# Up projection of a hybrid decoder layer: the low halo moves into the high row, and twelve matmuls of 258 columns become eight of 260 and four of 256

## The chip, the core and the metric

The kernel runs on one core of one Trainium2 chip. The metric is the device time of one execution in microseconds, as the median of several runs: 1258.69 us here (three runs, 1258.04 to 1259.17). Profiles are taken by the hardware profiler in an execution of their own.

## What is computed

One decoder layer for 1024 tokens and 16 meta tokens of width 1024, in float32. Ahead of the change stand the input projection, a convolution branch, windowed attention, their merge and a layer norm that gives `h`. The change lies in the feed-forward part:

```python
D_FF, FFN_TAPS = 2816, 3
up = causal_dwconv(h @ ffn_w_up, ffn_dw, ffn_dw_b)      # (T, 2 * D_FF), 3 taps along the tokens
u, g = jnp.split(up, 2, axis=-1)
f = (jax.nn.gelu(g, approximate=False) * u) @ ffn_w_down
return layer_norm(DEEPNORM_ALPHA * h + f, ln2_g, ln2_b)
```

The convolution is causal with 3 taps: an output at token t needs the projection at t, t - 1 and t - 2. A block of tokens therefore carries two extra columns in front, the halo.

## The kernel before

**Arithmetic.** Every float32 operand x is split into a high part, `hi = round(x)` to TensorE's reduced float32 format, and a low part, `lo = x - hi`. A product of two operands is three matmuls: high weight times high activation, high weight times low activation, low weight times high activation (`ah, hi`; `ah, lo`; `al, hi`). The weight is the stationary operand (128 x 128), the activation the moving one (128 channels x columns of tokens); the sum over channels is collected in PSUM.

**Up projection (the loop from L1550 on).** For each of 22 chunks `c` of 128 up channels and the 128 gate channels beside them, a 2 x 2 block product is made with seven block products instead of eight, the way Strassen and Winograd have it. The blocks of the weights are gate and up channels by the two halves of the 1024 contraction channels; the blocks of the activations are those halves by the two halves of the tokens. The seven moving operands (`B11, B21, BT2, BT4, BT1, BT3, B22`, sums and differences of the activation's blocks) are formed and split once and stay in SBUF; the seven weight operands are formed and split anew for every chunk, a few products ahead (`w_ahead(9)`, `wsplit` L1393 and L1394, sums in `up_weights` L1411).

A half of the tokens is 514 columns wide (`HW`): 2 of halo and 512. It is cut into two column groups, `SUB = [(0, 258), (258, 514)]`: group 0 has the halo and 256 tokens, group 1 has 256 tokens. Each of the seven products (`prod`, matmuls at L1572) goes over group 0 and then group 1: for each of four contraction chunks `k` the three terms `j`, so 12 matmuls of 258 columns and then 12 of 256. The four PSUM tiles `V4, X, Z, Y` (named pw, px, pz, py in the profile) have 1024 columns, two banks of 512 each; group 0 ends at column 512 and group 1 starts there, so that a half's 514 columns lie side by side at 254 to 768.

After each product ScalarE copies PSUM to SBUF (`copy`, L1584) or VectorE adds it to an earlier result (`tt`, L1580). This leaves `c11` (gate, first half of the tokens), `c12` (gate, second half), `c21` and `c22` (up). `conv_ffn` then makes the three taps: an ACTIVATE on ScalarE (L1499) for the newest tap and the bias, and two operations on VectorE (L1500, L1501) for the other two, of which the last ones read the halo. `gelu` (L1505) is on ScalarE, the product with `u` (L1509) on VectorE; the result goes to HBM.

The order of instructions on an engine is made by a list scheduler from priorities (`rank`) and from orders written out by hand (`after`, `line`). The first matmul of a group is put behind the last one of the group before (`last_mm`), so TensorE follows the text.

**First pass.** Chunk 0 goes over group 1 first and then over group 0 in a pass of its own, because group 0's operands are ready later: their tokens come from the last rows of the output projection before. `bsplit` makes a moving operand's two parts, the high one on ScalarE (L1264), the low one on VectorE (L1269); `bsub` (L1273) forms the sums. For B11 and B21 of group 0 this is done in two steps, columns 0 to 130 (`EARLY`) and 130 to 258 (`LATE`).

**Where the operands lie.** `B_AT` gives tile and offset of each operand; a part is four rows (one for each `k`), `BS = [260, 256]` elements apart, and the low rows follow the high ones. Group 0's operands lie in RHC, RHO, OA (four) and RX, group 1's in OC (four) and RHC (three).

**Down projection (L1717).** It begins when the last product of the up projection is out, with matmuls of 512 columns.

Of the kernel before, what the change touches and what calls it, by code (L numbers as in the profile page):

```python
# [25 lines left out]
AF = mybir.ActivationFunctionType  # L26
OP = mybir.AluOpType
AX = mybir.AxisListType

P = 128  # L30
D = 1024
KC = D // P
# [26 lines left out]

HW = 514  # L60
SUB = [(0, 258), (258, HW)]

W_LEN = 2304

BS = [260, 256]

ZA, ZN = 272, 768
OA_OO, OA_WO, OA_UP = (1144, 48, 7296), 120, 0
OC_CV, OC_UP = (1080, 7280, 0), 40
# [3 lines left out]
R_DN = 112  # L73
# [39 lines left out]
def tile_hybrid_layer(  # L113
# [3 lines left out]
    nc = tc.nc  # L117
# [38 lines left out]
    FA = arena.tile([P, 6144], F, name="FA")  # L156
    RHC = arena.tile([P, KC * T], R, name="RHC")
    RHO = arena.tile([P, KC * T], R, name="RHO")
# [21 lines left out]
    start = ExitStack()  # L180
# [363 lines left out]
    first = [weights([P, KC, P], in_cols(m)) for m in (4, 5, 0)]  # L544
# [288 lines left out]
    for h in range(NH):  # L833
        g, r = divmod(h, 4)
# [392 lines left out]
    def quadrant(sub, kk, h):  # L1227
        i = h * KC + kk * 4
        return FA[:, h1_at(sub, i):h1_at(sub, i + 4)]

    B_AT = [[(RHC, 40), (RHO, 4096 + 40)] + [(OA, OA_UP + i * KC * BS[0]) for i in range(4)] + [(RX, 56)],
            [(OC, OC_UP + i * 2048) for i in range(4)] + [(RHC, 4096 + R_DN), (RHC, 2048 + R_DN), (RHC, 6144 + R_DN)]]
    B11, B21, BT2, BT1, BT3, BT4, B22 = range(7)

    def bsum(sub, q, hl):
        n, s = SUB[sub][1] - SUB[sub][0], BS[sub]
        t, o = B_AT[sub][q]
        return t[:, o + hl * 4 * s:o + (hl + 1) * 4 * s].rearrange("p (k n) -> p k n", k=4)[:, :, :n]

    def bmat(sub, q, hl, k):  # L1240
        return bsum(sub, q, hl)[:, k]

    lined, high = [], []

    def line(ins):

        if lined:
            after(ins, lined[-1])
        lined.append(ins)
        return ins  # L1250
# [3 lines left out]
    def wide(x):  # L1254
        return x.rearrange("p (k n) -> p k n", k=4)
# [3 lines left out]

    def bsplit(sub, q, src, cs=slice(None)):  # L1260
        with rank(RK_SUMS):
            hi, lo = (bsum(sub, q, hl)[:, :, cs] for hl in range(2))
            src = wide(src)[:, :, cs]
            ins = nc.scalar.copy(hi, src)  # L1264
            if (sub, q) in ((0, BT2), (0, BT4), (0, BT1), (0, BT3)):
                if high:
                    after(ins, high[-1])
                high.append(ins)
            line(nc.vector.tensor_tensor(lo, src, f32(hi), OP.subtract))  # L1269

    def bsub(out, x, y, cs=slice(None)):
        with rank(RK_SUMS):
# [216 lines left out]
    def ftmp():  # L1489
        i = ft_next[0] % 8  # L1490
        ft_next[0] += 1
        return FA[:, i * 512:(i + 1) * 512]

    c11, c21, u2 = (FA[:, 4128 + i * HW:4128 + (i + 1) * HW] for i in range(3))
    c12, c22, u13 = (RT[:, i * HW:(i + 1) * HW] for i in range(3))

    def conv_ffn(cc, o):
        t = ftmp()
        nc.scalar.activation(t, cc[:, 2:HW], AF.Identity, bias=ffw(3, o), scale=ffw(2, o))  # L1499
        nc.vector.scalar_tensor_tensor(t, cc[:, 1:HW - 1], ffw(1, o), t, OP.mult, OP.add)  # L1500
        nc.vector.scalar_tensor_tensor(t, cc[:, 0:HW - 2], ffw(0, o), t, OP.mult, OP.add)  # L1501
        return t
# [47 lines left out]
    for c in range(FC):  # L1550
        V4, X, Z, Y = (pup.tile([P, 1024], F, name=n, tag=n) for n in ("pw", "px", "pz", "py"))
        passes = ((1,), (0,)) if c == 0 else ((0, 1),)
        for subs in passes:
            last = subs == passes[-1]
            w_next = iter(range(7))
            a, b = SUB[subs[0]][0], SUB[subs[-1]][1]

            def at(t):
                return t[:, 254 + a:254 + b]

            def prod(q, bank, first):
                if last:
                    w_ahead(9)
                    ah, al = w_ready.pop(0)
                else:
                    ah, al = w_ready[next(w_next)]
                for sub in subs:
                    o = bank[:, 254 + SUB[sub][0]:254 + SUB[sub][1]]
                    for k in range(4):
                        ks = slice(k * P, (k + 1) * P)  # L1570
                        for j, (x, hl) in enumerate(((ah, 0), (ah, 1), (al, 0))):
                            ins = nc.tensor.matmul(o, x[:, ks], bmat(sub, q, hl, k), start=first and k + j == 0,  # L1572
                                                   stop=k == 3 and j == 2, skip_group_check=not first)
                            if k + j == 0 and last_mm:
                                after(ins, last_mm[-1])
                    last_mm.append(ins)

            def tt(*x):
                with rank(RK_CHAIN):
                    return nc.vector.tensor_tensor(*x)  # L1580

            def copy(*x):
                with rank(RK_CHAIN):
                    copied.append(nc.scalar.copy(*x))  # L1584

            prod(B11, X, True)
            copy(u13[:, a:b], at(X))
            prod(B21, Z, True)
            if last and c not in (0, FH + 1):
                sums_load(c - 1 if c <= FH else c - 2)  # L1590
            tt(c11[:, a:b], at(Z), u13[:, a:b], OP.add)
            prod(BT2, X, False)
            copy(u2[:, a:b], at(X))
            if not last:
                turn(5, *last_rows, (V4, Z), last_mm, True)
                for q in (B11, B21):
# [274 lines left out]
```

## Time and profile before

| | |
|---|---|
| median of the runs | 1258.69 us |
| the profiled execution, whole | 1258.79 us |
| its span, first to last instruction | 1257.0 us |
| granted TensorE clock | 0.998 |
| TensorE busy (9176 matmuls) | 1243.3 us |
| weight loads busy | 1178.3 us |
| VectorE busy | 1076.1 us |
| ScalarE busy | 597.1 us |
| matmuls of the up projection (L1572) | 3696, from 602.9 to 1039.3 us |

An instruction's row has its line, engine and operation, the tiles it writes and reads (`out<-in`), partitions x elements, and the number of instructions merged into it. PE is TensorE, PEld its weight loads, DVE VectorE, ACT ScalarE. Matmuls overlap in TensorE's pipeline: a matmul's own length (some 280 ns for 256 columns) is a modelled one, and what it costs in a row of them is the distance from start to start. A bracket at the end of a row tells how long the engine had been idle and what ended that. The chain of waits is followed back from the last instruction to what released it.

### The profile page before, as it was taken

Reading aid. Unit: us, or ns where it says so; the run is one execution under the profiler, and the core shown is the slowest. Engines: PE = TensorE matmul, PEld = TensorE weight load, DVE = VectorE, ACT = ScalarE, POOL = GpSimd, SP = SyncE. Lnnn points to the kernel's source line nnn. Section 1 sums busy time; section 2 is a strip of 40 time slices with the busy share of each in tenths; the row PEclk is TensorE's granted clock in tenths of the full one; section 3 lists DMA queues with packets and bytes.
Section 4 is the critical chain, followed back from the end, with each engine's and each line's share of the span. In section 5 each row is a group of like instructions: output and inputs, shape, how many; then the busy total and the mean of one; then the engine's idle time right before and its main releaser. Section 6 shows DMA issues by size and latency. Waiting matters only on the chain.

```text
span 1257.0 us, 23022 instructions
## 1 busy us (share of the span) xinstructions
PE 1243.3 (99%) x9176; PEld 1178.3 (94%) x9176; DVE 1076.1 (86%) x1855; ACT 597.1 (48%) x1108; POOL 7.4 (1%) x8
## 2 busy tenths in 40 slices
PE   9999999999999999999999999999999999999997
PEld 8999999999999999788899999999999998888886
DVE  8989999999978677548899999998989977896697
ACT  8433264655474233344655555455555544445330
POOL 0000000001000000000000000000000000000000
PEclk9999999999999999999999999999999999999999
DMA  6393633422256554222145545454454566998712
GB/s 260 118 299 102 186 89 104 116 81 85 73 156 187 168 154 110 84 101 85 51 171 199 190 177 205 162 207 149 157 199 160 199 226 251 394 346 334 276 60 84
DMA packets 98685, 212.19 MB, mean 169 GB/s; under 512 B 11395, under 2 KB 38595, under 8 KB 98322
## 3 DMA queue, kind: packets, MB, share of 16 engines
q1 hardware_dynamic: 84414, 199.57, 46.6%
q10 hardware_dynamic: 14164, 11.15, 2.8%
q8 instruction: 72, 1.18, 0.4%
q14 instruction: 35, 0.29, 0.1%
HBM read 150.29 MB, written 62.70 MB: 169 GB/s over the span
## 4 chain that ended last, share of the span: by engine, by line
PE 96%; DVE 2%; ACT 1%; DMA 0%; issue 0%; DVEq 0%; SPq 0%; ACTq 0%
PE px L1572 15%; PE py L1572 10%; PE ps_x L1717 9%; PE ps_z L339 8%; PE ps_z L342 8%; PE ps_z L343 8%; PE ps_z L1717 7%; PE ps_p L1171 7%; PE pz L1572 5%; PE pw L1572 5%; PE ps_w L343 2%; PE ps_w L342 2%; PE ps_w L339 2%; PE ps_z L574 2%; PE ps_t L942 1%; PE ps_s L918 1%
## 5 line engine op out<-in xcount | busy, mean ns | idle before, releaser
L339 PE MATMUL ps_z<-RHO,w 128*128 128x256 f32 (+2 forms) x864 | 243.3, 282 | 0.0
L342 PE MATMUL ps_z<-RHO,w 128*128 128x256 f32 (+2 forms) x864 | 242.5, 281 | 0.0
L343 PE MATMUL ps_z<-RHC,w 128*128 128x256 f32 (+2 forms) x864 | 242.4, 281 | 0.0
L342 PEld LDWEIGHTS ps_z<-RHO,w 128*128 128x128 f32 x864 | 162.5, 188 | 0.5
L343 PEld LDWEIGHTS ps_z<-RHC,w 128*128 128x128 f32 x864 | 162.8, 188 | 0.2
L339 PEld LDWEIGHTS ps_z<-RHO,w 128*128 128x128 f32 x864 | 162.6, 188 | 0.1
L748 DVE SCALAR_TENSOR_TENSOR FA<-cin,cdw,FA 128x1026 f32<-128x1026 f32 x120 | 154.5, 1297 | 0.7
L1394 DVE TENSOR_TENSOR RHO<-wr,RHO 128x512 fp32r<-128x512 f32 x94 | 64.1, 690 | 8.0 <-ACT RHO L1393 7.9
L299 ACT CAST w<-wr 128x1024 fp32r<-128x1024 f32 x37 | 38.8, 1048 | 63.4 <-PE ps_z L343 49.9
L1393 ACT CAST RHO<-wr 128x512 fp32r<-128x512 f32 x94 | 56.9, 620 | 24.6 <-DVE wr L1411 12.4
L1411 DVE TENSOR_TENSOR wr<-wr 128x512 f32<-128x512 f32 x88 | 60.8, 691 | 0.1
L757 ACT ACTIVATE FA<-ps_z,colr 128x258 f32<-128x258 f32 (+1 forms) x64 | 30.1, 472 | 60.1 <-PE ps_z L343 52.5
L302 DVE TENSOR_TENSOR w<-wr,w 128x1024 fp32r<-128x1024 f32 x37 | 45.1, 1218 | 8.1 <-ACT w L299 7.9
L1584 ACT COPY FA<-px 128x514 f32<-128x514 f32 (+2 forms) x23 | 13.2, 573 | 78.7 <-PE px L1572 78.7
L1171 PE MATMUL ps_p<-OC,w 128*128 128x256 f32 (+1 forms) x384 | 48.1, 278 | 0.0
L1171 PE MATMUL ps_p<-OA,w 128*128 128x256 f32 (+1 forms) x384 | 47.8, 278 | 0.0
L1171 PEld LDWEIGHTS ps_p<-OC,w 128*128 128x128 f32 x384 | 46.2, 188 | 0.1
L1171 PEld LDWEIGHTS ps_p<-OA,w 128*128 128x128 f32 x384 | 45.9, 188 | 0.0
L1394 DVE TENSOR_TENSOR w<-wr,w 128x512 fp32r<-128x512 f32 x60 | 40.9, 690 | 5.7 <-ACT w L1393 5.6
L1572 PE MATMUL px<-OA,RHO 128*128 128x258 f32 x324 | 43.2, 282 | 0.0
L1499 ACT ACTIVATE FA<-OB,coll 128x512 f32<-128x512 f32 x44 | 35.9, 815 | 14.9 <-DVE OB L1580 14.9
L1572 PE MATMUL px<-OC,RHO 128*128 128x256 f32 x324 | 41.5, 277 | 0.8 <-DVE OB L1327 0.8
(450 smaller groups left out, 3082.0 us busy)
## 6 DMA issues: line engine op xcount, KB each, us to landing
wr<-in_w_up_dram SPq DMA_DIRECT2D x44, 512.0 KB, 3.6
wr<-in_w_z_dram SPq DMA_DIRECT2D x29, 512.0 KB, 4.1
OB<-in_w_down_dram SPq DMA_DIRECT2D x24, 512.0 KB, 4.8
fd<-FA SPq DMA_DIRECT2D x44, 256.0 KB, 2.0
FA<-sd SPq DMA_DIRECT2D x15, 512.0 KB, 8.9
qt<-qd SPq DMA_DIRECT2D x28, 256.0 KB, 4.3
OB<-td SPq DMA_DIRECT2D x14, 512.0 KB, 8.9
sgd<-FA ACTq DMA_DIRECT2D x48, 128.0 KB, 2.7
```

The costliest lines, as they stand in the source:

```text
L299: ins = nc.scalar.copy(hi, raw)
L302: return nc.vector.tensor_tensor(lo, raw, f32(hi), OP.subtract)
L339: ins = nc.tensor.matmul(ps, al, bh, start=i == 0, stop=False)
L342: nc.tensor.matmul(ps, ah, bh, start=False, stop=False)
L343: last = nc.tensor.matmul(ps, ah, bl, start=False, stop=i == n - 1)
L748: nc.vector.scalar_tensor_tensor(acc[c], cin[:, j:j + U], wc, acc[c], OP.mult, OP.add)
L1171: nc.tensor.matmul(ps[:, :b - a], x, rhs(k, hl, a, b), start=k + j == 0, stop=k == 3 and j == 2)
L1393: nc.scalar.copy(hi, src)
L1394: ins = nc.vector.tensor_tensor(lo, src, f32(hi), OP.subtract)
L1411: ins = nc.vector.tensor_tensor(*x)
L1572: ins = nc.tensor.matmul(o, x[:, ks], bmat(sub, q, hl, k), start=first and k + j == 0, stop=k == 3 and j == 2, skip_group_check=not first)
L1717: nc.tensor.matmul(banks[i], l[:, ts], r[:, ws], start=first and a and x + k == 0, stop=z and x == len(ops) - 1 and k == 2, skip_group_che ...
```

## The change

Group 0's two halo columns of the low part leave the low rows and stand in front of the high rows. A high row then has 260 columns (low halo 2, high halo 2, high 256), a low row 256 (no halo). The matmuls of group 0 are put in another order: four of 260 with the high weights, four of 260 with the low weights, four of 256 (low rows, high weights). Group 1's twelve of 256 follow unchanged in number and order. PSUM columns 252 and 253 now collect the halo's low part (with the high weights, and with the low weights too, a term that was left out before), 254 and 255 its high part.

So that the halves can be used as before, the copies and sums are 516 columns wide (`CU`), and `conv_ffn` first adds columns 0 and 1 to columns 2 and 3, each with an ACTIVATE of one column. `bsplit` writes the low rows of group 0 without the halo and the low halo with an operation of its own on 4 x 2 elements, where its columns begin at 0. Rows of group 0 are placed `HP = 264` elements apart (high) and 256 (low); in two of OA's four operands the low rows come first. 

```diff
+CU = HW + 2
...
+    HP = 264
+    B_AT = [[(RHC, 16, 0), (RHO, 4096 + 16, 0)] + [(OA, 8 + i * 2080, i % 2) for i in range(4)] + [(RX, 32, 0)],
+            [(OC, OC_UP + i * 2048, 0) for i in range(4)] + [(RHC, x + R_DN, 0) for x in (4096, 2048, 6144)]]
...
+    def row(sub, q, hl):
+        t, o, back = B_AT[sub][q]
+        hi = HP if sub == 0 else 256
+        o += (4 * 256 if back and not hl else 4 * hi if hl and not back else 0)
+        n = 256 if hl else hi
+        return t[:, o:o + 4 * n].rearrange("p (k n) -> p k n", k=4)
+
+    def bmat(sub, q, j, k):
+        if sub:
+            return row(1, q, j % 2)[:, k]
+        return row(0, q, j % 2)[:, k, 0:(260, 256, 260)[j]]
...
-            line(nc.vector.tensor_tensor(lo, src, f32(hi), OP.subtract))
+            n = src.shape[2]
+            a = cs.start or 0
+            x = 2 if sub == 0 and a == 0 else 0
+            a -= 2 if sub == 0 and a else 0
+            lo = bsum(sub, q, 1)[:, :, a:a + n - x]
+            line(nc.vector.tensor_tensor(lo, src[:, :, x:], f32(hi)[:, :, x:], OP.subtract))
+            if x:
+                line(nc.vector.tensor_tensor(row(0, q, 0)[:, :, 0:2], src[:, :, :2], f32(hi)[:, :, :2], OP.subtract))
...
     def conv_ffn(cc, o):
         t = ftmp()
+        for i in range(2):
+            nc.scalar.activation(cc[:, 2 + i:3 + i], cc[:, 2 + i:3 + i], AF.Identity, bias=cc[:, i:i + 1], scale=1.0)
+        cc = cc[:, 2:]
...
-                    o = bank[:, 254 + SUB[sub][0]:254 + SUB[sub][1]]
-                    for k in range(4):
-                        ks = slice(k * P, (k + 1) * P)
-                        for j, (x, hl) in enumerate(((ah, 0), (ah, 1), (al, 0))):
-                            ins = nc.tensor.matmul(o, x[:, ks], bmat(sub, q, hl, k), start=first and k + j == 0,
-                                                   stop=k == 3 and j == 2, skip_group_check=not first)
+                    terms = [(k, j) for k in range(4) for j in range(3)]
+                    if sub == 0:
+                        terms = [(k, j) for j in (0, 2, 1) for k in range(4)]
+                    for i, (k, j) in enumerate(terms):
+                        o = bank[:, 512:768] if sub else bank[:, (252, 256, 252)[j]:512]
+                        ins = nc.tensor.matmul(o, (ah, ah, al)[j][:, k * P:(k + 1) * P], bmat(sub, q, j, k),
+                                               start=first and i == 0, stop=i == 11, skip_group_check=not first)
```

More of the change, by code (lines that the diff above doesn't have):

```diff
@@ L1229, in quadrant @@
         return FA[:, h1_at(sub, i):h1_at(sub, i + 4)]
-    B_AT = [[(RHC, 40), (RHO, 4096 + 40)] + [(OA, OA_UP + i * KC * BS[0]) for i in range(4)] + [(RX, 56)],
-            [(OC, OC_UP + i * 2048) for i in range(4)] + [(RHC, 4096 + R_DN), (RHC, 2048 + R_DN), (RHC, 6144 + R_DN)]]
+    HP = 264
+    B_AT = [[(RHC, 16, 0), (RHO, 4096 + 16, 0)] + [(OA, 8 + i * 2080, i % 2) for i in range(4)] + [(RX, 32, 0)],
+            [(OC, OC_UP + i * 2048, 0) for i in range(4)] + [(RHC, x + R_DN, 0) for x in (4096, 2048, 6144)]]
     B11, B21, BT2, BT1, BT3, BT4, B22 = range(7)
     def bsum(sub, q, hl):
[L1236 to L1241, printed above, removed]
+        r = row(sub, q, hl)
+        return r[:, :, 2:260] if sub == 0 and not hl else r
+    def row(sub, q, hl):
[8 more added lines that the diff above has]
+        return row(0, q, j % 2)[:, k, 0:(260, 256, 260)[j]]
     lined, high = [], []
@@ L1261, in bsplit @@
         with rank(RK_SUMS):
-            hi, lo = (bsum(sub, q, hl)[:, :, cs] for hl in range(2))
             src = wide(src)[:, :, cs]
+            hi = bsum(sub, q, 0)[:, :, cs]
             ins = nc.scalar.copy(hi, src)
@@ L1492, in ftmp @@
         return FA[:, i * 512:(i + 1) * 512]
-    c11, c21, u2 = (FA[:, 4128 + i * HW:4128 + (i + 1) * HW] for i in range(3))
-    c12, c22, u13 = (RT[:, i * HW:(i + 1) * HW] for i in range(3))
+    c11, c21, u2 = (FA[:, 4128 + i * CU:4128 + (i + 1) * CU] for i in range(3))
+    c12, c22, u13 = (RT[:, i * CU:(i + 1) * CU] for i in range(3))
     def conv_ffn(cc, o):
         t = ftmp()
+        for i in range(2):
+            nc.scalar.activation(cc[:, 2 + i:3 + i], cc[:, 2 + i:3 + i], AF.Identity, bias=cc[:, i:i + 1], scale=1.0)
+        cc = cc[:, 2:]
         nc.scalar.activation(t, cc[:, 2:HW], AF.Identity, bias=ffw(3, o), scale=ffw(2, o))
@@ L1555, in tile_hybrid_layer @@
             w_next = iter(range(7))
-            a, b = SUB[subs[0]][0], SUB[subs[-1]][1]
+            a, b = SUB[subs[0]][0] + (2 if subs[0] else 0), SUB[subs[-1]][1] + 2
             def at(t):
-                return t[:, 254 + a:254 + b]
+                return t[:, 252 + a:252 + b]
             def prod(q, bank, first):
@@ L1567, in prod @@
                 for sub in subs:
-                    o = bank[:, 254 + SUB[sub][0]:254 + SUB[sub][1]]
-                    for k in range(4):
-                        ks = slice(k * P, (k + 1) * P)
-                        for j, (x, hl) in enumerate(((ah, 0), (ah, 1), (al, 0))):
-                            ins = nc.tensor.matmul(o, x[:, ks], bmat(sub, q, hl, k), start=first and k + j == 0,
-                                                   stop=k == 3 and j == 2, skip_group_check=not first)
-                            if k + j == 0 and last_mm:
-                                after(ins, last_mm[-1])
+                    terms = [(k, j) for k in range(4) for j in range(3)]
[5 more added lines that the diff above has]
+                                               start=first and i == 0, stop=i == 11, skip_group_check=not first)
+                        if i == 0 and last_mm:
+                            after(ins, last_mm[-1])
                     last_mm.append(ins)
```

## The prediction

> **What bounds the kernel now.** I read the page first: engines, then the chain that ended last.
>
> ```profile
> span 1257.0 us, 23022 instructions
> ...
> PE 1243.3 (99%) x9176; PEld 1178.3 (94%) x9176; DVE 1076.1 (86%) x1855; ACT 597.1 (48%) x1108; POOL 7.4 (1%) x8
> ...
> PE 96%; DVE 2%; ACT 1%; DMA 0%; issue 0%; DVEq 0%; SPq 0%; ACTq 0%
> ```
>
> TensorE is the last to finish nearly everywhere: 96% of the chain is its own work. So only time that TensorE's instructions take from each other counts, and I went on to the chain in order of time (start, length, what).
>
> ```profile
> 40.63 13.52 PE ps_z L574 x78
> ...
> 628.67 2.82 PE pz L1572 x24
> ...
> 755.28 2.81 PE py L1572 x24
> ...
> 1039.43 29.94 PE ps_z L1717 x132
> ```
>
> The up projection is L1572. Each piece there is one product over both column groups, 24 matmuls. From 628.67 to 755.28 are 45 pieces: 126.61 / 45 = 2.8136 us each, with nothing between them. The timeline of TensorE splits such a piece into its two halves (the second column is a modelled length; the starts are what counts).
>
> ```profile
> 684.79 1.61 PE L1572 MATMUL px<-RHC,RHO 128*128 128x258 f32 x12
> 686.24 1.53 PE L1572 MATMUL px<-OC,RHO 128*128 128x256 f32 x12
> 687.60 1.61 PE L1572 MATMUL pz<-RHO 128*128 128x258 f32 x12
> ...
> 704.48 1.61 PE L1572 MATMUL px<-RHC,w 128*128 128x258 f32 x12
> ```
>
> Twelve matmuls of 258 take 686.24 - 684.79 = 1.45 us, 120.8 ns each; twelve of 256 take 687.60 - 686.24 = 1.36 us, 113.3 ns each. Two columns more cost 7.5 ns. The chain's other pieces say how this goes on: a 512-wide matmul (L1717) takes 29.94 / 132 = 226.8 ns, twice a 256; a 384-wide one (L574, second token group) 13.52 / 78 = 173.3 ns. From 258 to 384 a column costs (173.3 - 120.8) / 126 = 0.417 ns, and from 384 to 512 (226.8 - 173.3) / 128 = 0.418 ns. So a column costs about 0.42 ns, and there is a step of some 6.7 ns (7.5 less two columns) that is paid once the width passes 256. All twelve matmuls of column group 0 pay it now.
>
> What of the rest could take over is read from a window over chunks 1 to 21 (columns: window, its length, then busy time and count of PE, weight loads, DVE, ACT, POOL):
>
> ```profile
> 625.80:1039.40 413.60, 413.60 (x3530) 413.60 (x3529) 376.87 (x602) 218.71 (x359) 0.00 (x0) 1.00 0.51 185
> ```
>
> VectorE is at 376.87 / 21 = 17.95 us a chunk, with (413.60 - 376.87) / 21 = 1.75 us left over; ScalarE has 194.89 / 21 = 9.3 us left. VectorE is the engine to watch.
>
> **The change part by part.**
>
> *Matmuls.* In group 0 the 12 matmuls of 258 become 8 of 260 (high rows with both weight parts) and 4 of 256 (low rows, high weights); group 1 keeps 12 of 256. Same count, same weight loads. The trace has no 260. By the slope it costs 120.8 + 2 x 0.417 = 121.7 ns. Below, it can hardly be under a 258 (120.8). Above, the line drawn from 256 through 258 would give 113.3 + 4 x 3.75 = 128.3, but the 384 and 512 rows show that the step is paid once and not per column, so I take 121.7. A product over both groups then takes 8 x 121.7 + 16 x 113.3 = 2786.7 ns, against 12 x 120.8 + 12 x 113.3 = 2810 by the same prices (unrounded ones): 23.3 ns less. There are 22 x 7 = 154 products, 7 of them in chunk 0: 154 x 23.3 = 3.59 us. With a 260 at a 258's price it is 30 ns and 4.62 us. The transition from wide to narrow stays at one a product, so the 3.6 ns by which the piece (2813.6) exceeds 2810 stays too.
>
> *Order inside a product.* High rows with high weights, high rows with low weights, then low rows: each matmul loads its weights before and after (9176 loads for 9176 matmuls), so no load is saved or added; nothing.
>
> *Halo on ScalarE.* Each conv_ffn gets two in-place additions of one column (128x1, bias a column of the tile) ahead of its wide ACTIVATE; 8 a chunk, 176 in all. Nearest rows of the groups by form:
>
> ```profile
> L1186 ACT ACTIVATE pair<-OB 128x2 fp32r<-128x2 f32 x7 | 1.4, 204 | 24.3 <-DVE OB L1184 24.3
> ...
> L477 ACT ACTIVATE t<-t,r 32x1 f32<-32x1 f32 x3 | 0.9, 293 | 0.1
> ...
> L1187 DVE SCALAR_TENSOR_TENSOR pair<-OB,pair 128x2 fp32r<-128x2 f32 x7 | 1.1, 158 | 1.1 <-ACT pair L1186 1.1
> ```
>
> Between 0.204 (immediate operands) and 0.293 us (a column as operand, in place); I take 0.293, whose operands are alike: 2.3 us a chunk, into 9.3 free. What they delay is the wide ACTIVATE behind them, hence VectorE's L1500, and the casts and PSUM copies queued after it. Timelines of ACT and DVE of one chunk:
>
> ```profile
> 648.47 0.59 ACT L1584 COPY OB<-px 128x514 f32<-128x514 f32 x1 [0.41 <-PE px L1572]
> ...
> 655.05 0.82 ACT L1499 ACTIVATE FA<-FA,coll 128x512 f32<-128x512 f32 x1
> ...
> 664.07 0.81 ACT L1499 ACTIVATE FA<-OB,coll 128x512 f32<-128x512 f32 x1
> ```
> ```profile
> 656.50 0.76 DVE L1500 SCALAR_TENSOR_TENSOR FA<-FA,coll 128x512 f32<-128x512 f32 x1
> ...
> 666.89 0.75 DVE L1500 SCALAR_TENSOR_TENSOR FA<-OB,coll,FA 128x512 f32<-128x512 f32 x1
> ```
>
> The gate's first conv (c11) is the tightest: its ACTIVATE ends at 655.87 and VectorE takes the result at 656.50, 0.63 us later, working on other things meanwhile; two additions are 0.59. For c22 the room is 666.89 - 664.88 = 2.0 us. A PSUM copy that slips by 0.59 still frees px in time: it ends at 649.06, and TensorE writes px again at 651.19:
>
> ```profile
> 651.19 2.81 PE px L1572 x24
> ```
>
> That is 2.1 us. So nothing of it reaches TensorE; without this cover it is the slow rival below. The copies and sums grow from 514 to 516 columns: 4 VectorE operations a chunk, two columns each at 0.69 us for 512, 0.003 us each; nothing.
>
> *Splits in the first pass.* The seven group 0 splits each lose two columns of four rows on VectorE (1032 to 1024) and gain one operation on 4 x 2 elements, at 0.158 us by L1187: up to 1.1 us in all. Two of them (the early parts of B11 and B21) fall before 602, where VectorE waits 1.44 us for TensorE anyway. Five fall into the stretch in which VectorE feeds TensorE directly:
>
> ```profile
> 602.17 0.69 DVE L1327 TENSOR_TENSOR OB<-ps_w,OB 128x512 f32<-128x512 f32 x1 [1.44 <-PE ps_w L343]
> ...
> 615.35 1.23 DVE L1269 TENSOR_TENSOR OA<-OB,OA 128x1032 fp32r<-128x1032 f32 x1
> ...
> 618.09 2.37 DVE L1269 TENSOR_TENSOR OA<-FA,OA 128x1032 fp32r<-128x1032 f32 x2
> ...
> 620.98 1.23 DVE L1269 TENSOR_TENSOR OA<-FA,OA 128x1032 fp32r<-128x1032 f32 x1
> 622.12 1.23 DVE L1269 TENSOR_TENSOR RX<-FA,RX 128x1032 fp32r<-128x1032 f32 x1
> ```
> ```profile
> 618.36 1.69 PE L1572 MATMUL px<-OA,RHO 128*128 128x258 f32 x12
> ...
> 622.78 1.59 PE L1572 MATMUL px<-OA,w 128*128 128x258 f32 x12
> 624.21 1.62 PE L1572 MATMUL py<-RX,w 128*128 128x258 f32 x12
> ```
>
> BT3's low part is ready at 622.21 and used at 622.78, B22's at 623.35 and 624.21. Four small operations ahead of the first, five ahead of the second, are 0.6 and 0.8 us if none overlaps, while TensorE comes some 0.1 us earlier: a wait of about 0.1 to 0.2 us, from nothing to 1.1 us at the ends. The first matmul must now also wait for the small operation, since the low halo sits in the high row. I let chunk 0 earn nothing: its seven products' 0.16 us go there.
>
> *Placement.* Rows move by some elements inside the same tiles, 264 apart instead of 260; no DMA, no load and no queue changes.
>
> **The sum.** 147 products x 23.3 ns = 3.43 us, on TensorE's own path up to L1717, which follows without a gap. The profiled execution took 1258.79 us (its span 1257.0 and 1.8 around it), 0.1 over the median of the runs shown (1258.69). 1258.79 - 3.43 = 1255.36; against the median, 1255.3. That is 0.27%; 0.2%, about what a measurement of this kernel can tell from no change, is 2.5 us.
>
> **The rivals.**
>
> *Part of it is given back in chunk 0.* All seven small operations come to lie on the path: 1.1 us, 1255.3 + 1.1 = 1256.4. For it: VectorE has no idle time there between 610 and 625. Against it: the margins above, 0.57 and 0.86 us.
>
> *Columns have one price.* If the 7.5 ns belonged to the switching between two widths and not to the width, only columns would count: 8 x 260 + 16 x 256 = 6176 instead of 6168, 8 x 0.443 (113.3 / 256) = 3.5 ns more a product, 0.5 us more in all: 1259.2. For it: widths alternate every twelve matmuls here. Against it: L574's 384 and L1717's 512 stand in long rows of one width and carry the same step.
> The Trainium skill, "TensorE: Matmul & The Clock Gate", section "Back-to-back issue gap", says as much: N / 2.4 + 2.5 ns for a warm array, so 110.8 for a 260 and 109.2 for a 256, which would make the change a loss of 0.5 us. The trace disagrees with it: 113.3, 120.8, 173.3 and 226.8 ns stand where it gives 109.2, 110.0, 162.5 and 215.8.
>
> *The step comes from how rows lie.* Rows of 258 stand 260 apart; if that cost the 6.7 ns, rows 264 apart would not, a 260 would cost 113.3 + 4 x 0.417 = 115.0, a product 2733 ns, 76.7 less: 11.8 us, 1246.9. Against it: the 512-wide rows pay twice a 256.
>
> *Slower: the additions make VectorE the bound.* Eight a chunk, in front of the four ACTIVATEs whose results VectorE waits for in its fixed order. They decide once they cost more than VectorE's 1.75 us, 0.22 us each. At 0.293 us, all of it exposed: 17.95 + 8 x 0.293 = 20.29 us a chunk against 19.70 now, 0.59 x 21 = 12.4 us, 1271. For it: VectorE is at 91% here, and the price is above 0.22. Against it: the rooms of 0.63 and 2.0 us, in which VectorE has other work.
>
> **How the numbers follow.** Forecast 0.73; given back in chunk 0 0.07; one price a column 0.07; rows 0.03; VectorE the bound 0.10. The time is the forecast's, 1255.3; its own bounds are 1254.07 (a 260 at a 258's price, all 154 products, 1258.69 - 4.62) and 1256.1 (five small operations exposed, 5 x 0.158 = 0.8 us). From 1254.0 to 1257.0 the range holds the first two cases, 0.80. Faster by over 0.2% (under 1256.17): the forecast and the rows, 0.76. Within: the next two, 0.14. Slower: 0.10.
>
> **What would show it.** In the chain after, a piece of 24 takes 2.790 us (2.784 if a 260 costs a 258's, 2.817 by one price a column, 2.737 by the rows). In the timeline eight 260s take 0.97 us and sixteen 256s 1.82 us. The waits of L1572's matmuls stay near what they are:
>
> ```profile
> its engine sat idle before it (us, times) until:
>   ACT FA L1374: 2.6, 2
>   DVE OB L1327: 2.0, 2
>   ACT OB L1584: 0.5, 2
> ```
>
> A new line for VectorE's splits (L1269) there would be chunk 0's rival. Pieces with gaps between them from chunk 1 on, with idle of VectorE before L1500 in every chunk, would be the slow one and would make the prediction wrong.

## The result: 1254.1 us, and where the 0.4% came from

| | before | after |
|---|---|---|
| median of five runs each | 1259.17 us (1258.04 to 1260.84) | 1254.09 us (1253.95 to 1255.29) |
| ratio | | 0.9961, 95% interval 0.9950 to 0.9972 |
| the profiled execution | 1258.79 us | 1255.0 us |
| its span | 1257.0 us | 1253.2 us |
| start to the first matmul of the up projection | 602.92 us | 603.51 us |
| chunk 0 (both passes) | 22.74 us | 22.70 us |
| chunks 1 to 21, 147 products | 413.60 us | 409.08 us |
| down projection to the end | 217.70 us | 217.91 us |

The last four rows are the distances between the first matmuls of the stages in the two traces. The changed stage lost 4.52 us. The stages before and behind it, which the change doesn't touch, were 0.59 and 0.21 us longer in this execution; that is why the two spans stand only 3.8 us apart.

In the changed kernel the up projection's matmuls are L1594 (L1572 before), the additions L1518, the wide ACTIVATE L1520, the taps L1521 and L1522, the copies L1606, the sums L1602, the splits L1285 and their small operation L1287. The page's row of engines and the shares of its chain:

```profile
PE 1239.1 (99%) x9176; PEld 1173.8 (94%) x9176; DVE 1078.1 (86%) x1862; ACT 627.4 (50%) x1284; POOL 7.4 (1%) x8
...
PE 96%; DVE 2%; ACT 1%; DMA 1%; issue 0%; SPq 0%; DVEq 0%; ACTq 0%
```

TensorE is the bound as before, with the same 9176 matmuls and 4.2 us less time in them. The chain of waits in order of time, one chunk of it:

```profile
801.69 2.79 PE px L1594 x24
804.48 2.79 PE pz L1594 x24
807.26 2.79 PE px L1594 x24
810.05 2.77 PE pw L1594 x24
812.82 2.77 PE py L1594 x24
815.60 2.79 PE px L1594 x24
...
821.17 2.79 PE px L1594 x24
```

A chunk takes 821.17 - 801.69 = 19.48 us, 2.783 a product where it was 2.814. Over the stage that is (413.60 - 409.08) / 147 = 30.7 ns a product, not 23.3. And the products are of two sorts: pw (BT4) and the py behind it (BT1) are 13 ns shorter than the other five. These two are the ones whose low rows lie in front of the high rows. TensorE's timeline, cut so that the four narrow matmuls of group 0 have a row of their own:

```profile
684.65 1.59 PE L1594 MATMUL px<-RHC,RHO 128*128 128x260 f32 x12
...
687.43 1.59 PE L1594 MATMUL pz<-RHO 128*128 128x260 f32 x12
...
693.01 1.58 PE L1594 MATMUL pw<-OA,RHO 128*128 128x260 f32 x12
...
695.78 1.58 PE L1594 MATMUL py<-OA,RHO 128*128 128x260 f32 x12
```
```profile
685.60 0.63 PE L1594 MATMUL px<-RHC,RHO 128*128 128x256 f32 x4
686.07 1.41 PE L1594 MATMUL px<-OC,RHO 128*128 128x256 f32 x11
```
```profile
693.96 0.62 PE L1594 MATMUL pw<-OA,RHO 128*128 128x256 f32 x4
694.42 0.62 PE L1594 MATMUL pw<-RHC,RHO 128*128 128x256 f32 x4
```

(A row of x12 holds eight of 260 and four of 256 here, under the first one's form.) In px the eight of 260 take 685.60 - 684.65 = 0.95 us, 119 ns each. The four of 256 take 0.47 us, 118 ns each, though the twelve of 256 behind them, up to 687.43, take 113.3 each. So one width has two prices inside one product, and a 260 costs hardly more than a narrow one beside it. In pw the four take 694.42 - 693.96 = 0.46 us, some 114 ns each, and the twelve behind them 113.3 again.

What the change added is hidden. The additions' group, one chunk of ScalarE and VectorE at the gate's first conv, the window of chunks 1 to 21 (the fifth number behind the window is ScalarE's busy time: 248.80 us where 218.71 stood), and TensorE's idle time before L1594:

```profile
L1518 ACT ACTIVATE FA<-FA 128x1 f32<-128x1 f32 x88 | 21.0, 285 | 3.8 <-DVE FA L1602 3.8
```
```profile
655.59 0.48 ACT L1518 ACTIVATE FA<-FA 128x1 f32<-128x1 f32 x2
655.97 0.81 ACT L1520 ACTIVATE FA<-FA,coll 128x512 f32<-128x512 f32 x1
```
```profile
656.86 0.74 DVE L1521 SCALAR_TENSOR_TENSOR FA<-FA,coll 128x512 f32<-128x512 f32 x1
```
```profile
626.40:1035.40 409.00, 409.00 (x3529) 409.00 (x3528) 378.74 (x603) 248.80 (x530) 0.00 (x0) 1.00 0.52 187
```
```profile
  ACT FA L1392: 2.6, 2
  DVE OB L1345: 2.0, 2
  ACT OB L1606: 0.5, 2
```

An addition is 285 ns long, and the next instruction starts 0.19 us behind it ((655.97 - 655.59) / 2). Two of them take 0.38 us at c11, where 0.63 were free. The ACTIVATE ends at 656.78 and VectorE takes its result at 656.86, so 0.08 us of room is left there; the other 0.17 us went with a shift of the work around it. TensorE's three idle entries are the same three, with the same times.

### The profile page after: what moved, and what is told of

Same layout as the page of the kernel before. It is cut to its first block, busy times and chain, and to the rows that moved or that the text cites. A ratio compares the mean times of both kernels' runs of the same rounds, so it can differ in the third digit from the quotient of the medians.

```text
span 1253.2 us, 23194 instructions
## 1 busy us (share of the span) xinstructions
PE 1239.1 (99%) x9176; PEld 1173.8 (94%) x9176; DVE 1078.1 (86%) x1862; ACT 627.4 (50%) x1284; POOL 7.4 (1%) x8
## 4 chain that ended last, share of the span: by engine, by line
PE 96%; DVE 2%; ACT 1%; DMA 1%; issue 0%; SPq 0%; DVEq 0%; ACTq 0%
PE px L1594 15%; PE py L1594 10%; PE ps_x L1739 9%; PE ps_z L340 8%; PE ps_z L343 8%; PE ps_z L344 8%; PE ps_z L1739 7%; PE ps_p L1172 7%; PE pz L1594 5%; PE pw L1594 5%; PE ps_w L344 2%; PE ps_w L343 2%; PE ps_w L340 2%; PE ps_z L575 2%; PE ps_t L943 1%; PE ps_s L919 1%
## 5 line engine op out<-in xcount | busy, mean ns | idle before, releaser
L1606 ACT COPY FA<-px 128x516 f32<-128x516 f32 (+2 forms) x23 | 13.1, 571 | 71.2 <-PE px L1594 71.2
L1594 PE MATMUL px<-OA,RHO 128*128 128x260 f32 x324 | 43.0, 282 | 0.0
L1594 PE MATMUL px<-OC,RHO 128*128 128x256 f32 x324 | 41.2, 276 | 0.8 <-DVE OB L1345 0.8
L1594 PE MATMUL px<-RHC,RHO 128*128 128x256 f32 (+1 forms) x312 | 40.6, 279 | 0.1
```

The source lines that it names most:

```text
L1594: ins = nc.tensor.matmul(o, (ah, ah, al)[j][:, k * P:(k + 1) * P], bmat(sub, q, j, k), start=first and i == 0, stop=i == 11, skip_group_ch ...
```

## The experiments

All but two run the whole layer, and each is an edit of the changed kernel unless it says otherwise. Lengths of products are distances from first matmul to first matmul, the median over chunks 1 to 21.

### Does the order of the rows in memory make the two sorts?

`e1_high_first` lays all operands high rows first:

```diff
-... [(OA, 8 + i * 2080, i % 2) for i in range(4)] ...
+... [(OA, 8 + i * 2080, 0) for i in range(4)] ...
```

> Low rows behind the high rows in all seven operands of group 0 (in the changed kernel BT4 and BT1 have them in front, and their pieces of 24 matmuls take 2.774 us, the other five 2.787). The high rows of BT4 and BT1 now begin where their low rows began; both places are 32 bytes past a multiple of 256 in the program's allocation, so the phase of the high rows stays and the low rows move from 32 to 160. Theory 'order in memory': BT4 and BT1 rise to 2.787, a chunk from 19.480 to 19.506 us, 0.55 us over 21 chunks. Rival 'phase of the high rows': they stay at 2.774 and the chunk at 19.480.

```profile
692.92 1.59 PE L1594 MATMUL pw<-OA,RHO 128*128 128x260 f32 x12
694.35 1.53 PE L1594 MATMUL pw<-RHC,RHO 128*128 128x256 f32 x12
695.72 1.59 PE L1594 MATMUL py<-OA,RHO 128*128 128x260 f32 x12
```

pw takes 695.72 - 692.92 = 2.80 us: longer than the 2.774 it had, but also longer than the 2.787 of the other five, which stay. One execution took 1256.59 us, beside 1258.25 of the kernel before. So the two operands do react to where their rows lie, but "high first" isn't the price, and both theories missed: 2.787 and 2.774 were expected.

`e2_low_first` lays all seven low rows first:

```diff
-    B_AT = [[(RHC, 16, 0), (RHO, 4096 + 16, 0)] + [(OA, 8 + i * 2080, i % 2) ...] + [(RX, 32, 0)],
+    B_AT = [[(RHC, 16, 1), (RHO, 4096 + 16, 1)] + [(OA, 8 + i * 2080, 1) ...] + [(RX, 32, 1)],
```

> Low rows in front in all seven operands; the high rows of the other five keep their phase (160 bytes past a multiple of 256), their low rows move from 32 to 160. Theory 'order in memory': all seven pieces take 2.774 us, a chunk 19.416, 1.3 us less over 21 chunks. Rival 'phase of the high rows': nothing changes, 2.787 and 2.774, 19.480 a chunk.

```profile
686.15 1.59 PE L1594 MATMUL px<-RHC,RHO 128*128 128x260 f32 x12
687.58 1.57 PE L1594 MATMUL px<-OC,RHO 128*128 128x256 f32 x12
688.99 1.59 PE L1594 MATMUL pz<-RHO 128*128 128x260 f32 x12
...
696.07 1.52 PE L1594 MATMUL pw<-RHC,RHO 128*128 128x256 f32 x12
697.43 1.58 PE L1594 MATMUL py<-OA,RHO 128*128 128x260 f32 x12
```

Both theories missed. B11, BT2 and BT3 take 2.842 us, B21, BT4 and B22 2.798, BT1 2.773. A chunk takes 19.69 us, all that the change had gained is gone, with every matmul of the change in place (one time: 1260.53 us). The most telling rows are those of group 1, which the edit doesn't touch: its twelve of 256 take 688.99 - 687.58 = 1.41 us in px, 117.5 ns each, and 697.43 - 696.07 = 1.36 in pw. The price of a matmul depends on what ran before it, and it can stay for twelve in a row.

### Does the order of the matmuls, or the width of the low weights' columns?

`e3_k_outer` brings back the old order in group 0 (`k` outside, the three terms inside) with the new widths:

```diff
-                    if sub == 0:
-                        terms = [(k, j) for j in (0, 2, 1) for k in range(4)]
```

> The old order inside a product: for each k a 260 (high weights), a 256 (low rows), a 260 (low weights), instead of eight 260 and then four 256. Theory 'a matmul has a price by its own width': the pieces stay at 2.787 and 2.774, the sum does not ask for the order. Rival 'switching between widths costs': eight switches more a product at the 1.6 ns that the piece of the kernel before (2813.6 against 2810 by the widths, two switches) leaves for one: 2.800, 0.27 us a chunk less 0.18 of noise-free doubt, 1.9 us over 21 chunks.

```profile
803.93 2.81 PE px L1592 x24
...
812.38 2.84 PE pw L1592 x24
```

A chunk takes 19.72 us: 2.813 for most products, 2.837 for BT4, 1259.9 us in one execution. Eight of 260 and four of 256, as the prediction counted them, are worth nothing in the old order at these places.

`e4_258` takes the low halo out of the low weights' matmuls, so that four of the eight wide ones have 258 columns (the low weights' product with the low halo is left out, as in the kernel before):

```diff
-        return row(0, q, j % 2)[:, k, 0:(260, 256, 260)[j]]
+        return row(0, q, j % 2)[:, k, (0, 0, 2)[j]:(260, 256, 260)[j]]
...
-                        o = ... bank[:, (252, 256, 252)[j]:512]
+                        o = ... bank[:, (252, 256, 254)[j]:512]
```

> Low weights over 258 columns instead of 260 (the low weights times the low halo are left out, as in the kernel before). Theory '0.417 ns a column above the step': four matmuls 0.83 ns cheaper, 3.3 ns a piece, 0.023 us a chunk, 0.5 us over 21. Rival 'a 260 costs what a 258 costs': no difference, 19.480 a chunk.

Fewer columns, and longer: B11, BT2 and BT3 2.839 us, B21 and B22 2.787 as in the change, BT4 2.801, BT1 2.773. A chunk takes 19.67 us, and one execution took 1260.53 us. The rows begin 8 bytes further on. So widths, order and memory order each shift the price, by up to 63 ns a product (BT4 in e3), and none of them explains the others' shifts. What is common to the four edits is that they move where the moving rows begin, or what comes before what.

### The price by place, measured alone

`e5_places` is a program of matmuls alone; nothing of the layer is computed. For five widths, four places of the weights and 16 to 64 places of the moving rows (16 bytes apart) it runs 36 matmuls in a row. Weights and moving rows change within a stream, but only by multiples of 256 bytes (`RUN` is 36, `w` and `m` are the places in bytes, the sums count elements of 4 bytes):

```python
for r in range(RUN):
    k = r % 4
    t = r % 8
    wo = w0 + w // 4 + t * 128
    mo = a0 + m // 4 + k * 768
    nc.tensor.matmul(bank[:, 0:n], W[:, wo:wo + 128], A[:, mo:mo + n], start=False, stop=False)
```

> A program of matmuls alone, nothing of the layer: 368 streams of 36 matmuls of one width (256, 258, 260, 384, 512 columns), the moving rows beginning m bytes and the weights w bytes past a multiple of 1 KB (m in steps of 16, w = 0, 32, 96, 160; for 256 columns and w = 0 m up to 1 KB), each between matmuls of 512. Theory 'price by width alone': 113.3, 120.8, 121.7, 173.3 and 226.7 ns whatever m and w. Rival 'the moving rows and the weight load of the next matmul get in each other's way, by their places': the time of one width changes with m, repeats when m goes on by 256 and follows m - w; 256 has places at 113.3 and at 117.7 ns (both are seen in the second run's sixteen 256s), and 260 has places near 113.3 x 260 / 256 = 115.1 ns.

Two streams of 256 columns in the timeline, with the moving rows 80 and 112 bytes past the weights:

```profile
45.02 4.48 PE L57 MATMUL n256w0m<-A,W 128*128 128x256 f32 x36
49.33 0.39 PE L58 MATMUL n256w0m<-A,W 128*128 128x512 f32 x1
```
```profile
55.96 4.28 PE L57 MATMUL n256w0m<-A,W 128*128 128x256 f32 x36
60.08 0.39 PE L58 MATMUL n256w0m<-A,W 128*128 128x512 f32 x1
```

The first stream takes (49.33 - 45.02) / 36 = 119.7 ns a matmul, the second (60.08 - 55.96) / 36 = 114.4; without its first twelve the second settles at 113.3. Same width, same clock, other place. The mean of the last 24 of each stream:

| columns | shortest | longest |
|---|---|---|
| 256 | 113.3 ns | 120.0 ns |
| 258 | 116.7 | 122.4 |
| 260 | 118.3 | 121.8 |
| 384 | 173.3 | 180.2 |
| 512 | 226.7 | 236.7 |

With the weights at 0 the list of 256 columns repeats every 256 bytes up to 1 KB, within 0.1 ns but for two places of the first 256 bytes (0.5 and 2.0 ns off). With the weights moved by 32 or 96 bytes it is the same list shifted by as much, two of sixteen places apart; at 160 five of sixteen differ, by 2 to 5 ns. So the price goes mostly by where the moving row begins relative to the weights, modulo 256 bytes, but one place can settle at more than one price.

From the addresses in the programs: the weights of the up projection begin 96 bytes past a multiple of 256 in all kernels here, and group 1's rows 32 past one. The kernel before has its group 0 rows at 0 or 128, 260 elements apart, so that each row begins 16 bytes further along. The change puts its first wide row at 160 (the next ones 32 bytes further along each) and the low rows at 32 for five operands, and both at 32 for BT4 and BT1. That is the difference between the two sorts. Group 1 stands 192 bytes past the weights (32 - 96, modulo 256), where a stream of 256 alone takes 117.8 ns; in the change it runs at 113.3. What runs before must matter too.

`e6_sequences` therefore runs whole products, group 0 and then group 1, each four times in a row. It keeps the weights and group 1 at the kernels' places and varies the place and spacing of group 0's rows (432 placements; again nothing of the layer):

```python
for j, wt in ((0, ah), (2, al)):                       # the change's order, st = 264, 260, 268
    ops += [(ps_t[:, 252:512], wt[k], A[:, ho + k * st:ho + k * st + 260]) for k in range(4)]
ops += [(ps_t[:, 256:512], ah[k], A[:, lo + k * 256:lo + k * 256 + 256]) for k in range(4)]
```

> Matmuls alone again: whole products (24 matmuls in the changed kernel's order, weights 96 and narrow group-1 rows 32 bytes past a multiple of 256, as there), four times each, with the wide rows 264, 260 or 268 apart and begun at one of 16 places, the low rows at one of 8; and 48 products in the order of the kernel before. Theory 'place': the places of the kernels give again what they give there: wide 160 and low 32: 2.787 us; wide 32, low 32: 2.774; wide 32, low 160: 2.800; wide 160, low 160: 2.798 or 2.842; the old order, 260 apart, wide 0 or 128: 2.813. Among 384 products some are under 2.774, and if the wide rows reach 118.3 ns (the best 260 of the streams) with all narrow ones at 113.3, the best is 2.760. Rival 'price by width, with something of the layer's other engines in it': without the other engines all new products take one time, 2.787.

It gives back the kernels' prices: 2.787 us for wide rows at 160 with low rows at 32, 2.773 for 32 and 32, 2.800 for 32 and 160 (e1's two), 2.813 for the old order at 0 or 128. (e3's and e4's products, with their mixed widths, are not among its placements.) With both at 160 (e2's) the same 24 matmuls at the same places alternate. L66 is group 0, L70 group 1:

```profile
974.54 1.59 PE L66 MATMUL ps_s<-A,W 128*128 128x260 f32 x12
975.97 1.57 PE L70 MATMUL ps_s<-A,W 128*128 128x256 f32 x12
977.39 1.59 PE L66 MATMUL ps_s<-A,W 128*128 128x260 f32 x12
978.81 1.53 PE L70 MATMUL ps_s<-A,W 128*128 128x256 f32 x12
980.18 1.59 PE L66 MATMUL ps_s<-A,W 128*128 128x260 f32 x12
```

The first product's group 1 takes 1.42 us, the second one's 1.37. This is e2's alternation, without the layer and its other engines. The program also takes turns with two sets of weights (4 KB apart) and four PSUM tiles, which could alternate as well; but in six placements the first price comes back with the fourth repetition, which has other weights and another PSUM tile than the first (wide rows at 80, 264 apart, low rows at 160: 2.842, 2.815, 2.783, 2.842 us). So what ran before counts, and not the buffer alone.

Over all its placements (the mean of the last three of the four repetitions) the change's order ranges from 2.760 to 2.887 us a product, with a median of 2.813. The old order (48 placements) ranges from 2.787 (260 apart, from 144 on) to 2.878, with a median of 2.818. So at a typical place the two orders are 5 ns apart, and the sixteen placements of the old order with rows 260 apart, as the kernel before has them, have a median of 2.813 too: no difference. The kernel before stood near the middle of its range, at 2.813; the change as drawn stands, at 2.783, among the better tenth (2.793). Best place against best place the change's matmuls are worth 27 ns a product, as far as this search goes: it tried the old order at 48 placements against 384, with its low rows only right behind the high ones, and neither with group 1 or the weights elsewhere. A better place for the old order isn't excluded.

### What hides the additions, and how much of it there is

`e7_no_additions` leaves out the two additions of each conv, so the low halo's share is missing from the first two tokens of a block:

```diff
-        for i in range(2):
-            nc.scalar.activation(cc[:, 2 + i:3 + i], ..., bias=cc[:, i:i + 1], scale=1.0)
```

> The changed kernel without conv_ffn's two one-column additions (the low halo's part is left out of the output). Theory 'hidden': pieces of 2.787 and 2.774 us with no gaps as before, TensorE's time from the first to the last product unchanged within 0.1 us; ScalarE's busy time falls by 176 x 0.28 = 49 us. Rival 'the additions cost something': the up projection gets shorter by more than 0.3 us.

The chunks 1 to 21 take 409.079 us, to the last digit what they take with the additions (409.079), and the whole 1254.09 us in one execution. ScalarE's time in the window falls back to 220.31:

```profile
626.40:1035.40 409.00, 409.00 (x3525) 408.82 (x3525) 376.84 (x601) 220.31 (x360) 0.00 (x0) 1.00 0.52 188
```

`e8_more_additions` puts four more one-column operations behind the two, 24 a chunk in place of 8, on columns that nothing reads any more:

```diff
+        for i in (0, 1, 0, 1):
+            nc.scalar.activation(cc[:, i:i + 1], cc[:, i:i + 1], AF.Identity, bias=eps, scale=1.0)
```

> Six operations of one column ahead of each conv instead of two (the four new ones work on the two columns that nobody reads any more): 24 a chunk instead of 8, at about 0.19 us from start to start. Theory 'the cover ends between': VectorE waits before L1521 in every chunk, c11's ACTIVATE comes 6 x 0.19 = 1.1 us later where 0.6 were free; 16 x 0.19 = 3.0 us more a chunk on ScalarE fit into its 7.6 us free, and VectorE's 1.4 us of slack a chunk swallow most of 4 x 0.5 us: between nothing and 0.6 us a chunk, 0 to 13 us in all. Rival 'there is room for three times as many': no gap in TensorE, the time of the changed kernel.

What TensorE waited for ahead of its matmuls (L1596 there; L1608 is the copy; its two other entries stay), and a piece of its chain:

```profile
  ACT OB L1608: 3.1, 9
```
```profile
807.49 2.88 PE px L1596 x24
```

The stage takes 411.31 us, 2.23 more, and the whole 1256.46 us. VectorE's wait for the wide ACTIVATE grows too, to 2.8 us in nine waits, but what ends TensorE's idle time is the copy out of PSUM: nine times, where there were two. The median product is unchanged. The chain behind four of these waits, which make products 0.4 to 0.7 us longer, runs through ScalarE's additions and wide ACTIVATEs, in two of them behind a load of weights that took over 5 us. So the cover seems to end somewhere between 8 and 24 operations a chunk. One execution can't put the whole 2.2 us down to the additions: e1, e3 and e10 each lose 0.7 to 0.9 us to one wait for a copy too, without one addition more than the change (e10 has none), behind a load of weights (`DMA wr<-in_w_up_dram`) of 6.0 to 7.1 us.

### With the places chosen

`e10_before_placed` is the kernel before with nothing but group 0's rows at 144 (OA is 48 elements longer for it):

```diff
-    B_AT = [[(RHC, 40), (RHO, 4096 + 40)] + [(OA, OA_UP + i * KC * BS[0]) for i in range(4)] + [(RX, 56)],
+    B_AT = [[(RHC, 12), (RHO, 4096 + 12)] + [(OA, 4 + i * 2112) for i in range(4)] + [(RX, 28)],
```

> The kernel before, with 12 matmuls of 258 and 12 of 256 in its own order and the halo where it was; only group 0's rows begin elsewhere, 144 bytes past a multiple of 256 (260 apart as they were). Theory 'place': the product program's 2.787 us a piece instead of 2.813, a chunk 19.507, 4.0 us less over 21 chunks and some 0.2 in chunk 0: about 1255.0 us, nearly the changed kernel's time without any of the change. Rival 'width': 2.813 and the time of the kernel before.

```profile
686.38 1.59 PE L1572 MATMUL pz<-RHO 128*128 128x258 f32 x12
687.80 1.52 PE L1572 MATMUL pz<-OC,RHO 128*128 128x256 f32 x12
689.16 1.59 PE L1572 MATMUL px<-OA,RHO 128*128 128x258 f32 x12
```

A product takes 689.16 - 686.38 = 2.78 us (2.787 in the median), with twelve of 258 at some 119 ns. Five runs: 1255.32 us (1254.52 to 1256.23), ratio 0.9969, 0.9958 to 0.9981. The changed kernel beside it, seven runs, as `e11_change_again`: 1254.88 us, ratio 0.9967, 0.9956 to 0.9978.

> The changed kernel as it is, on the same chip as the two before it: 2.783 us a piece on the mean, 1254.1 us, so that the three stand beside each other.

The intervals lie on each other. In the median product 26 ns come without anything of the change but the places, where the change has 30.7 on the mean. Chunks 1 to 21 take 410.37 us, 3.24 less than before, and not 4.52: a part of the difference is one product that waited 0.7 us longer, for a copy out of PSUM.

`e9_change_placed` is the change with the wide rows of all seven at 176 and the low ones at 32 (offsets of high and low rows are given separately, OA is 48 elements longer here too):

```diff
+    B_AT = [[(RHC, 1108, 48), (RHO, 5204, 4144), (OA, 12, 1064), (OA, 3148, 2088), (OA, 4236, 5288),
+             (OA, 7372, 6312), (RX, 1060, 0)],
```

> The changed kernel with the same matmuls in the same order; only the places of group 0's rows are others: all seven operands have their wide rows begin 176 and their low rows 32 bytes past a multiple of 256. Theory 'place': the product program's 2.760 us for every piece, a chunk 19.320 us instead of 19.480, 3.36 us less over 21 chunks and 0.1 to 0.2 in chunk 0: about 1250.7 us against 1254.1, ratio to the kernel before 0.993. Rival 'width alone': no difference, 1254.1.

```profile
685.64 1.56 PE L1595 MATMUL pz<-RHO 128*128 128x260 f32 x12
687.04 1.52 PE L1595 MATMUL pz<-OC,RHO 128*128 128x256 f32 x12
688.40 1.56 PE L1595 MATMUL px<-OA,RHO 128*128 128x260 f32 x12
...
823.65 1.69 PE L1595 MATMUL px<-OA,RHO 128*128 128x260 f32 x12
```

688.40 - 685.64 = 2.76 us, as e6 had it: the four narrow ones are at 113.3 now, the eight wide ones at 118.3. Chunks 1 to 21 take 405.85 us, 7.7 less than before. All of the products there are at 2.760 but for one or two in an execution (the one at 823.65 takes 2.88). The whole doesn't follow as cleanly: of twelve runs six lie at 1250.5 to 1251.9 us and six at 1255.5 to 1265.2. The median is 1253.7 us; the ratio over all twelve is 0.9974, with 0.9950 to 0.9999 (that of the medians would be 0.9959). So by these runs this version isn't shown to be better than the change as drawn. `e12_placed_again` was to catch a long one in a profile:

> The placed kernel once more, for its profile: seven of its twelve executions took 1250.5 to 1251.9 us, the other five 1255.5 to 1265.2, which no kernel here did before. If this one is a long one, its trace says where: in the up projection, as pieces over 2.760 us (the stream has fallen into another rhythm), or behind it (the 512-wide matmuls at more than 226.8 ns), or in a stage that the edit does not touch. If it is a short one, the pieces are 2.760 us again and the question stays open.

It took 1251.73 us, a short one again (and the count in its expectation is off by one: six and six). What makes the long executions stays open, as does whether they come from these places at all: in 19 runs beside it the kernel before kept to 1258.0 to 1261.0.

## Why the prediction was right in time, and which of its steps were not

**The bound.** Right: TensorE is 96% of the chain, before and after, and the time came out of its own matmuls.

**What is hidden.** Right, in each part. The additions cost nothing (e7), and c11 has indeed little room: 0.08 us is left where 0.63 were. Their price per conv was smaller, 0.38 us and not 0.59, since they overlap. The slow rival fell. Something of its mechanism exists, but not where it was put: in the one execution with three times the additions (e8) it is the PSUM copy that comes late, and the stage is 2.2 us longer.

**Chunk 0.** Right: it earns 0.05 us. The splits' small operations take 0.15 us each, and those of BT3 and B22 are done before TensorE's matmuls with them start at 623.35 and 624.78:

```profile
622.91 0.15 DVE L1287 TENSOR_TENSOR OA<-FA,OA 128x8 fp32r<-128x8 f32 x1
...
624.13 0.15 DVE L1287 TENSOR_TENSOR RX<-FA,RX 128x8 fp32r<-128x8 f32 x1
```

The rival that gave part of it back there fell with that.

**The matmuls' term.** 23.3 ns a product were predicted and 30.7 measured; 7.4 x 147 = 1.1 us. The sum 8 x 121.7 + 4 x 113.3 = 1427 even stands in the trace for group 0 of five products (686.07 - 684.65 = 1.42 us), but by two errors that cancel: the wide ones take 119, the narrow ones 118. What was short: the 3.6 ns that was to stay went (group 1 now takes its 12 x 113.3 from the first matmul on), and the two products with both parts at 32 earn 13.3 more, 13.3 x 2 / 7 = 3.8 over all. 23.3 + 3.6 + 3.8 = 30.7.

The measured 2.783 us a product and 1254.09 us also stand right on the prediction's other bound, "a 260 at a 258's price" (2.784 and 1254.07). That is a coincidence: that bound has eight matmuls at 120.8 and all sixteen narrow ones at 113.3; the trace has the eight at 119, and in five products of seven it has four of the narrow ones at 118.

**The steps that failed.** Three, and they hang together. "Placement", with "no DMA, no load and no queue changes", was costed at nothing; e1, e2 and e10 show that places alone move a product by up to 55 ns (B11 in e2; 26 in e1 and e10), more than the term itself. "Order inside a product", also at nothing, fell with e3: with the old order at the same places the change earns nothing. And the step of some 6.7 ns "that is paid once the width passes 256" isn't one of width alone. At one place, 192 bytes past the weights, e5 has 117.8 for a 256 and 120.8 for a 258, 3.0 ns apart; 7.5 was the distance between a 258 at a middling place and a 256 in a sequence that had settled at its best. The prediction saw 384 and 512 columns fit one line through 258 and took this as proof; those rows lie at their own places, and e5 has a spread of 7 and 10 ns for these widths. The timeline of the kernel before already held a warning, two rows behind the ones that the prediction read:

```profile
690.41 1.60 PE L1572 MATMUL px<-OA,RHO 128*128 128x258 f32 x12
691.85 1.54 PE L1572 MATMUL px<-OC,RHO 128*128 128x256 f32 x12
693.23 1.61 PE L1572 MATMUL pw<-OA,RHO 128*128 128x258 f32 x12
```

In this product (BT2) the twelve of 258 take 1.44 us and the twelve of 256 take 1.38, where B11 has 1.45 and 1.36: the same widths in the same kernel at two prices each.

**The rival of the rows** (chance 0.03) had the right kind of cause and the wrong size: it let the step vanish for rows 264 apart, 76.7 ns. The best of 384 placements is worth 53 ns against the kernel before (2.813 to 2.760).

**One price a column** fell as well, as a forecast of no change. The Trainium skill's rule beside it ("TensorE: Matmul & The Clock Gate", section "Back-to-back issue gap") gives 109.2 ns for 256 columns, for an isolated matmul, which the prediction didn't say. No stream of e5 came below 113.3, and the runs decide.

So the time was right mostly by luck. The prediction counted the matmuls rightly, but the count doesn't carry the time: e2 and e3 have the same eight of 260 and four of 256, and their chunks 1 to 21 take 413.55 and 414.91 us, nothing less than the 413.60 before. The change gains because its places, in its order, happen to be good ones. That the changed kernel, places and all, is 4.5 us shorter in the up projection is shown. That the widths and the order are worth anything as such holds only best place against best place as far as they were searched, 27 ns a product, about 4 us; at typical places it is 5 ns, 0.7 us, or nothing.

## What to carry to other kernels

Where TensorE is back to back with loads and matmuls, the start of the moving rows against the weights, modulo 256 bytes, belongs to a change as much as its widths do: before an edit that moves rows is credited or blamed for anything, run the old kernel with its rows moved too. A price per matmul that is read from one stream holds for that place and that sequence, and a difference of a few ns between two widths may be one of places. A short program that runs the sequence at every place costs one run and tells what the best of the places tried is for each variant. Whether the whole kernel follows has still to be measured: e9's did in six of twelve executions.

## What the runs showed of the hardware

- A matmul of 256 columns takes 113.3 to 120.0 ns from start to start at full clock, 512 columns 226.7 to 236.7, by the place of the moving row relative to the weights modulo 256 bytes. What in the hardware makes it so, no run here shows.
- The price has a memory. Twelve matmuls of 256 at unchanged places ran at 117.5 ns behind some products and at 113.3 behind others (e2), and the same product, at the same places modulo 256 bytes, alternates between 2.842 and 2.798 us when it is repeated (e6).
- One-column ACTIVATEs of 285 ns follow each other at 190 ns.
- The kernel with the shortest up projection has the widest spread over executions (1250.5 to 1265.2 us); its cause is open.
